# Transposing q and k whole in float32 and splitting them on the way out of PSUM, with keys of four blocks in one tile

## The chip, the cores and the metric

The kernel runs on one core of one Trainium2 chip. The metric is the device time of one execution in microseconds, the median over runs. The kernel before has a median of 1172.38 us in three runs (1171.7 to 1174.79 us).

## The reference, cut to what matters

One decoder block on 1024 tokens of width 1024. A modulated RMS norm feeds one input projection; its columns are split into queries, keys and values of two mixers. Mixer A has 8 query heads on 2 key heads with a window of 128 and a sink; mixer B has 8 heads, each the mixture of three dilated windows. Both outputs are normed and go through one output projection; then a squared-ReLU MLP follows. Everything is float32.

```python
h = rms_norm(x, g_attn_pre[l]) * (1 + sc_a) + sh_a
proj = h @ w_in[l]
qa = partial_rope(proj[..., :o1].reshape(b, s, A_Q_HEADS, HEAD_DIM), cos, sin)
ka = partial_rope(proj[..., o1:o2].reshape(b, s, A_KV_HEADS, HEAD_DIM), cos, sin)
va = proj[..., o2:o3].reshape(b, s, A_KV_HEADS, HEAD_DIM)
qb = partial_rope(proj[..., o3:o4].reshape(b, s, B_HEADS, HEAD_DIM), cos, sin)
kb = partial_rope(proj[..., o4:o5].reshape(b, s, B_HEADS, HEAD_DIM), cos, sin)
vb = proj[..., o5:].reshape(b, s, B_HEADS, HEAD_DIM)
oa = banded_attention(qa.reshape(b, s, A_KV_HEADS, A_GROUP, HEAD_DIM), ka, va, A_WINDOW - 1, sink=sink_a[l])
ob = dilated_mixture_attention(qb, kb, vb).reshape(b, s, B_W).astype(x.dtype)
mixed = jnp.concatenate([rms_norm(oa, g_mix_a[l]), rms_norm(ob, g_mix_b[l])], axis=-1)
y = mixed @ w_out[l]
x = x + gt_a * rms_norm(y, g_attn_post[l])
h = rms_norm(x, g_mlp_pre[l]) * (1 + sc_m) + sh_m
y = jnp.square(jax.nn.relu(h @ w_up[l])) @ w_down[l]
x = x + gt_m * rms_norm(y, g_mlp_post[l])
```

The scores are `q · k / 8` (head width 64); the kernel computes a window's scores with a mask that is added to them.

## The kernel before

**Split numbers.** A float32 number is held as a high part in the matmul's reduced type (`fp32r`) and a low part, the rest. A projection product takes three matmuls (high by high, high by low, low by high; L766, L767, L769). For the scores the two parts of q stand one above the other on the 128 partitions, 64 for the high and 64 for the low part of one head, and are the stationary operand; the keys' high part stands twice on the 128 partitions, and so does their low part. So two matmuls, one with the keys' high and one with their low parts, give the whole product.

**Stages.** From 0 to about 60 us the modulation is computed, x is normed and transposed, and the first projection unit begins. From about 61 to 455 us projection and attention run interleaved. Then come the output projection, and from about 545 us the MLP, which is the longest part (L1797 to L1799).

**Units and tiles.** The input projection has six units of 384 columns: units 0 to 3 hold two heads of mixer B each (2 q, 2 k, 2 v), units 4 and 5 one key head of mixer A each (4 q, 1 k, 1 v). Each unit runs over 8 token blocks of 128, so there are 48 tiles. A tile is 24 matmuls of 384 columns into a PSUM bank `pj` (`acc` in unit 0). `evac(u, tb, ...)` takes it from there:

- `f_vh`, `f_vl`: v is split (ACT, then DVE);
- `f_rope`: the rotary part, on DVE, in the bank itself;
- `f_h`, `f_l`: q and k are split in token order, high parts on ACT (L706, L707), low parts on DVE (L711, L712), into `sp` and `sk`; the bank is then free;
- `f_pq`: q goes through transposes in `fp32r`, one for each head (L719), into the PSUM bank `px`; `f_q` copies each out on ACT, times -1/8 (L724);
- `f_pk`: k goes through two transposes a head (L731) into `px` again; `f_k` copies them out to a key tile `kt` on ACT or DVE, whichever the planner expects to end earlier (L745). In units 4 and 5 each key block is copied a second time for the next block's tile (L756).

So a tile has six transposes in two groups, and `px`, a single bank, is taken twice. A key tile holds 256 keys: two blocks in units 0 to 3, the block before and its own in units 4 and 5.

**Attention items.** `s_b` does the scores of a pair of query blocks of one B head (all keys so far, in PSUM pieces of up to 512 and matmuls of up to 256 columns, L1022), `s_a_` those of one query block of four A heads (L1073). Then DVE adds the mask and takes the minimum (L1040, L1089), ACT takes the exponential (L1047, L1094), the probabilities are scaled (L1052 on POOL, L1111 on POOL or DVE), transposed in float32 (L1125, L1128, L1132), split (L1139 on ACT, L1143 on DVE) and multiplied by v (L1156 to L1161, L1167).

**What sets the order.** No order is written out. `Sched` plans while the program is built: each step has a duration in the source (`t_ps`, `t_dv`, a number), dependencies, and counted resources (`r_x` for the bank `px`, `r_k` and `r_q` for key and query buffers). It places steps on five in-order queues at the times that it expects; PE takes its streams in the order of `prefer()`, transposes of q and k (`post`) first. On the chip the queues run in that order, whatever the durations turn out to be. So a changed duration or resource in the source moves instructions on all engines.

## Time and profile before

| what | value |
|---|---|
| median of the runs | 1172.38 us |
| the profiled execution's own time | 1175.14 us |
| its span, first to last instruction | 1173.3 us |
| granted TensorE clock, mean | 0.993 |
| PE busy, by the page | 1137.0 us, 97% |
| DVE, ACT, POOL busy, by the page | 74%, 58%, 20% |
| stretch of projection and attention | about 61 to 455 us |

How to read it: the execution's time is 1.84 us over its span, and it is 2.76 us over the median of the runs. A matmul's duration in the trace includes its way through the array, so that one starts before the one ahead has ended; what a matmul costs in a row of others is the distance from one start to the next, and that is read from the timeline. PE's busy share therefore tells when PE waits, not how fast it works.

### The profile page before, as it was taken

To read this page: it belongs to the slowest core of one execution; us is meant where nothing else is said; L and a number is where in the kernel's file an instruction comes from. 1 tells how busy PE (TensorE), PEld (TensorE's weight loads), DVE (VectorE), ACT (ScalarE), POOL (GpSimd) and SP (SyncE) were. 2 spreads that over 40 slices of the span, in tenths; PEclk is the share of its full clock that TensorE was granted. 3 is DMA by queue.
4 is the path that set the end of the run, shared out by engine and by line. 5 is a ranking of instruction groups with operands and counts; after the bars stand their busy time and mean duration, and the time that the engine had idled before them with its cause. 6 is when DMAs were issued, how large, how long until landed. Compare 5 with 4: busy or idle time off the path is not lost.

```text
span 1173.3 us, 17394 instructions
## 1 busy us (share of the span) xinstructions
PE 1137.0 (97%) x6042; PEld 987.6 (84%) x6042; DVE 871.9 (74%) x1765; ACT 677.6 (58%) x1421; POOL 239.3 (20%) x295
## 2 busy tenths in 40 slices
PE   8999999999999999999899999999999999999996
PEld 7889999999988878887688888888888888888885
DVE  7876787776788896668969764499653796636998
ACT  7966676666666786666667524473225733246542
POOL 2053464554654451112000000000000000000002
PEclk9999999999999999999999999999999999999998
DMA  9712234132223224465485147922258411575103
GB/s 327 209 64 78 74 87 117 53 104 71 70 70 104 79 73 130 172 202 218 150 333 181 36 150 243 357 84 90 100 214 306 143 50 54 202 283 201 37 19 144
DMA packets 96488, 166.54 MB, mean 142 GB/s; under 512 B 11408, under 2 KB 48400, under 8 KB 96400
## 3 DMA queue, kind: packets, MB, share of 16 engines
q1 hardware_dynamic: 96400, 165.42, 42.0%
q8 instruction: 48, 0.79, 0.3%
q14 instruction: 40, 0.33, 0.1%
HBM read 137.08 MB, written 28.31 MB: 141 GB/s over the span
## 4 chain that ended last, share of the span: by engine, by line
PE 77%; DVE 11%; issue 4%; ACT 3%; POOL 1%; DMA 1%; DVEq 0%; POOLq 0%; SPq 0%; ACTq 0%
PE mlp_ps L1798 16%; PE mlp_ps L1799 16%; PE mlp_ps L1797 16%; PE pj L766 4%; PE pj L767 4%; PE pj L769 4%; PE s_ps L1022 3%; PE o_ps L1156 2%; PE pt_ps L1125 1%; DMA w_st<-in_w_in 1%; PE y_ps L1373 1%; PE y_ps L1375 1%; PE y_ps L1374 1%; PE s_ps L1073 1%; PE pt_ps L1128 1%
## 5 line engine op out<-in xcount | busy, mean ns | idle before, releaser
L1797 PE MATMUL mlp_ps<-hw 128*128 128x512 f32 x896 | 349.7, 390 | 1.1 <-ACT hw L1559 1.1
L1798 PE MATMUL mlp_ps<-hw 128*128 128x512 f32 x896 | 348.7, 389 | 1.1 <-DVE hw L1565 1.1
L1799 PE MATMUL mlp_ps<-hw 128*128 128x512 f32 x896 | 348.6, 389 | 0.0
L1797 PEld LDWEIGHTS mlp_ps<-hw 128*128 128x128 f32 x896 | 168.2, 188 | 36.9 <-ACT hw L1559 1.6
L1798 PEld LDWEIGHTS mlp_ps<-hw 128*128 128x128 f32 x896 | 168.2, 188 | 36.6 <-DVE hw L1565 1.4
L1799 PEld LDWEIGHTS mlp_ps<-hw 128*128 128x128 f32 x896 | 168.2, 188 | 34.9
L1568 DVE TENSOR_TENSOR hw<-w,hw 128x1024 fp32r<-128x1024 f32 x96 | 114.6, 1219 | 95.1 <-ACT hw L1561 93.0
L1561 ACT CAST hw<-w 128x1024 fp32r<-128x1024 f32 x96 | 97.4, 1046 | 129.9 <-PE mlp_ps L1799 93.2
L1897 POOL TENSOR_TENSOR st<-st,nhalf 128x1 f32<-128x1 f32 x8 | 7.7, 977 | 602.0 <-DVE st L1895 602.0
L766 PE MATMUL pj<-w_hl,hw 128*128 128x384 f32 x320 | 119.1, 372 | 0.0
L767 PE MATMUL pj<-w_hl,hw 128*128 128x384 f32 x320 | 108.7, 340 | 0.5 <-DVE w_hl L506 0.5
L769 PE MATMUL pj<-w_hl,hw 128*128 128x384 f32 x320 | 108.9, 340 | 0.0
L1561 ACT CAST hw<-u 128x1024 fp32r<-128x1024 f32 x48 | 48.6, 1052 | 64.6 <-PE mlp_ps L1799 64.6
L1143 DVE TENSOR_TENSOR ph<-pt_ps,ph 128x512 fp32r<-128x512 f32 (+1 forms) x110 | 68.9, 644 | 18.6 <-ACT ph L1139 18.0
L1568 DVE TENSOR_TENSOR hw<-u,hw 128x1024 fp32r<-128x1024 f32 x48 | 57.0, 1218 | 18.2 <-ACT hw L1561 18.2
L1139 ACT CAST ph<-pt_ps 128x512 fp32r<-128x512 f32 (+1 forms) x110 | 59.8, 562 | 12.9 <-PE pt_ps L1128 8.8
L1052 POOL TENSOR_SCALAR p_sb<-p_sb,den 128x128 f32<-128x128 f32 (+3 forms) x64 | 49.1, 773 | 87.4 <-DVE den L1050 49.8
L1855 DVE TENSOR_TENSOR yacc<-yacc,mlp_ps 128x512 f32<-128x512 f32 x96 | 62.2, 681 | 3.3 <-PE mlp_ps L1799 3.3
L767 PEld LDWEIGHTS pj<-w_hl,hw 128*128 128x128 f32 x320 | 61.0, 191 | 2.1 <-DVE w_hl L506 0.8
L766 PEld LDWEIGHTS pj<-w_hl,hw 128*128 128x128 f32 x320 | 60.7, 190 | 1.6 <-issue 0.5
L769 PEld LDWEIGHTS pj<-w_hl,hw 128*128 128x128 f32 x320 | 60.6, 189 | 0.0
L1047 ACT ACTIVATE p_sb<-p_sb,mn 128x128 f32<-128x128 f32 (+3 forms) x64 | 50.0, 782 | 17.4 <-DVE mn L1040 13.5
(206 smaller groups left out, 2201.0 us busy)
## 6 DMA issues: line engine op xcount, KB each, us to landing
hw<-s_dram SPq DMA_DIRECT2D x84, 512.0 KB, 4.4
wa_st<-in_w_ada SPq DMA_DIRECT2D x32, 512.0 KB, 4.2
w<-in_w_up SPq DMA_DIRECT2D x32, 512.0 KB, 5.1
w<-in_w_down SPq DMA_DIRECT2D x32, 512.0 KB, 7.5
s_dram<-hw SPq DMA_DIRECT2D x28, 512.0 KB, 4.5
x_sb<-in_x SPq DMA_DIRECT2D x16, 512.0 KB, 5.4
wa<-in_w_ada SPq DMA_DIRECT2D x32, 256.0 KB, 6.1
w_st<-in_w_in SPq DMA_DIRECT2D x32, 192.0 KB, 3.8
```

Of the source, the lines that this page charges most:

```text
L766: T.matmul(ps, hw[:, tb, 0, t], w[:, 0], start=(k == 0), stop=False)
L767: T.matmul(ps, hw[:, tb, 0, t], w[:, 1], start=False, stop=False)
L769: T.matmul(ps, hw[:, tb, 1, t], w[:, 0], start=False, stop=(k == KC - 1))
L1047: A.activation(rec.p[qi], rec.p[qi], AF.Exp, bias=b["mn"][:, m:m + 1], scale=-1.0, accum_out=b["den"][:])
L1139: A.copy(b["ph"][:, 0, :w], b["pt"][:, :w])
L1143: V.tensor_tensor(b["ph"][:, 1, :w], b["pt"][:, :w], b["ph"][:, 0, :w].bitcast(F32), ALU.subtract)
L1561: A.copy(out[j][0], flat(src[j]))
L1568: V.tensor_tensor(out[j][1], flat(src[j]), out[j][0].bitcast(F32), ALU.subtract)
L1797: T.matmul(ps[m][:], sh, mh, start=starts and k == 0, stop=False, **kw)
L1798: T.matmul(ps[m][:], sh, ml_, start=False, stop=False, **kw)
L1799: T.matmul(ps[m][:], sl, mh, start=False, stop=k == 3, **kw)
L1855: e = op("DVE", t_dv(512), lambda: V.tensor_tensor(y(), y(), ps[m][:], ALU.add), [e, ml.e_y[tb, n]], gives=gives, prio=1)
```

## The change

**Transposes.** `f_h` now copies q and k of a tile in float32 to one buffer `sq`: three groups of 128 columns, each a pair of q heads, or one k head twice. `f_l` is gone. `f_pq` transposes the three groups in float32 into `px`, once. Out of PSUM, `f_q` copies the high parts of q on ACT (two instructions, 64 partitions each), `f_ql` the low parts on DVE, as a `scalar_tensor_tensor` whose output lies on the other 64 partitions (two instructions); `f_k` copies the keys' high parts on ACT, and `f_kl` takes the low parts on DVE, one instruction a k head each. `f_kn`, the second copy of A's keys, is gone. The bank `pj` is given free after this copy on ACT, and no longer after DVE's low parts of q and k.

**Scores.** A key tile holds four blocks, 512 keys (`kts[u, tb // 4, h]`). A B score product takes all of a piece's columns at once, up to 512. An A block finds its 256 keys side by side in a tile, but for block 4, whose two key blocks lie in two tiles: there each head takes four matmuls of 128 columns in place of two of 256.

**Planner.** Buffers are counted by the new tiles (`NK` 6 of twice the size, `NQ` 4 of four times), the duration of a dense projection step is 0.52 in place of 0.49, that of a score step 0.014 + 2 · max(0.1, 0.00043 · columns).

```diff
-    WR, WS, NP, NV, NK, NQ, NT, NO = 10, 5, 4, 21, 10, 12, 2, 6
+    WR, WS, NP, NV, NK, NQ, NT, NO = 10, 5, 4, 21, 6, 4, 2, 6
...
         def f_h():
-            t.sp = prp.tile([P, 4, 2, 64], F32R, name="sp", tag="sp", bufs=2)
-            t.sk = prp.tile([P, 2, 2, 2, 64], F32R, name="sk", tag="sk", bufs=2)
-            b["kd"] = b["prv"][:, nq:].unsqueeze(2).to_broadcast([P, nk, 2, 64])
-            A.copy(t.sp[:, :nq, 0], b["prv"][:, :nq])
-            A.copy(t.sk[:, :nk, 0], b["kd"])
-        e5 = op("ACT", t_as(64 * nq) + t_as(128 * nk), f_h, [e3], takes=[(r_sp, 1)], prio=2)
-
-        def f_l():
-            V.tensor_tensor(t.sp[:, :nq, 1], b["prv"][:, :nq], t.sp[:, :nq, 0].bitcast(F32), ALU.subtract)
-            V.tensor_tensor(t.sk[:, :nk, 1], b["kd"], t.sk[:, :nk, 0].bitcast(F32), ALU.subtract)
-        e6 = op("DVE", t_dv(64 * nq) + t_dv(128 * nk), f_l, [e5, t.e_v], gives=[(r_bank, 1)], prio=2)
+            t.sq = prp.tile([P, 3, 2, 64], F32, name="sq", tag="sq", bufs=2)
+            A.copy(t.sq[:, :n2], b["prv"][:, :nq].rearrange("p (x e) d -> p x e d", e=2))
+            A.copy(t.sq[:, n2:n2 + nk], b["prv"][:, nq:].unsqueeze(2).to_broadcast([P, nk, 2, 64]))
+        e5 = op("ACT", t_as(64 * nq) + t_as(128 * nk), f_h, [e3, t.e_v], takes=[(r_sp, 1)], gives=[(r_bank, 1)], prio=2)
...
-            b["pq"] = px.tile([P, 4, P], F32R, name="pq", tag="x")
-            for h in range(nq):
-                T.transpose(b["pq"][:, h], t.sp[:, h].rearrange("p s d -> p (s d)"), ident_r[:])
-        e7 = pe_op("post", 0.056 * nq, f_pq, [e6, e_idr], takes=[(r_x, 1), (r_q, nq)])
+            b["pq"] = px.tile([P, 3, P], F32, name="pq", tag="x")
+            for x_ in range(3):
+                T.transpose(b["pq"][:, x_], t.sq[:, x_].rearrange("p e d -> p (e d)"), ident)
+        e7 = pe_op("post", 0.327, f_pq, [e5], takes=[(r_x, 1), (r_q, int(new_q)), (r_k, nk if new_k else 0)], gives=[(r_sp, 1)])
...
         def f_q():
-            for h in range(nq):
-                A.mul(t.q[h][:], b["pq"][:, h].bitcast(F32), -0.125)
-        t.e_q = op("ACT", nq * t_ps(128), f_q, [e7], gives=[(r_x, 1)], prio=2)
+            for e in range(2):
+                src, dst = of(0, e)
+                A.mul(dst[64 * e:64 * e + 64], src, -0.125)
+        eq = op("ACT", 2 * t_ps(128 * n2), f_q, [e7], prio=2)
+
+        def f_ql():
+            for e in range(2):
+                src, dst = of(0, e)
+                V.scalar_tensor_tensor(dst[64 - 64 * e:128 - 64 * e], src, -0.125,
+                                       dst[64 * e:64 * e + 64].bitcast(F32), ALU.mult, ALU.subtract)
+        t.e_q = op("DVE", 2 * t_dv(128 * n2), f_ql, [eq], prio=2)
...
-        e8 = pe_op("post", 0.112 * nk, f_pk, [e6], takes=[(r_x, 1), (r_k, need_k)], gives=[(r_sp, 1)])
...
+        ek = op("ACT", nk * t_ps(128), f_k, [e7], prio=2)
+        t.e_k = op("DVE", nk * t_dv(128), f_kl, [ek, t.e_q], gives=[(r_x, 1)], prio=2, after=posted)
...
-            d = dense(0.49, emit, [w_e[u, k]] + [], takes=[(r_pj, 1)] if k == 0 else [], gives=gives, after=tick)
+            d = dense(0.52, emit, [w_e[u, k]] + [], takes=[(r_pj, 1)] if k == 0 else [], gives=gives, after=tick)
...
-                    for b0 in range(0, cw, 256):
-                        w = min(256, cw - b0)
-                        for hl in range(2):
-                            T.matmul(s[:, b0:b0 + w], toks[u, qb].q[h][:],
-                                     kts[u, (c0 + b0) // 256, h][:, hl, :w], start=(hl == 0), stop=(hl == 1))
-                d = 0.218 * -(-cw // 256)
+                    for hl in range(2):
+                        T.matmul(s[:, :cw], toks[u, qb].q[h], kts[u, m, h][:, hl, :cw], start=(hl == 0),
+                                 stop=(hl == 1))
+                d = 0.014 + 2 * max(0.1, 0.00043 * cw)
...
-                kt = kts[u, qb, 0]
+                x_ = qb % 4
+                keys = [(qb // 4, 0 if x_ == 0 else (x_ - 1) * P, x_ * P + P, k0 if x_ else P)]
+                if x_ == 0 and qb:
+                    keys.append((qb // 4 - 1, 3 * P, 4 * P, 0))
                 for hh in range(2):
-                    for hl in range(2):
-                        T.matmul(s[:, hh, k0:], toks[u, qb].q[2 * j + hh][:], kt[:, hl, k0:],
-                                 start=(hl == 0), stop=(hl == 1))
+                    for i_, a_, z_, o_ in keys:
+                        for hl in range(2):
+                            T.matmul(s[:, hh, o_:o_ + z_ - a_], toks[u, qb].q[2 * j + hh], kts[u, i_, 0][:, hl, a_:z_],
+                                     start=(hl == 0), stop=(hl == 1))
```

**Where instructions move.** The rows below are the programs' own, in their order on one engine. First PE in unit 3, around the transposes of q and k of token block 4, before: `pq` and `pk` are the two groups of transposes, `pj` the projection, `pt_ps` the probabilities' transposes.

```order
L1022 MATMUL s_ps<-kt,qt 128x256 x4
L719 MATMUL pq<-ident_r,sp 128x128 x2
L766 MATMUL pj<-w_hl,hw 128x384
L767 MATMUL pj<-w_hl,hw 128x384
L769 MATMUL pj<-w_hl,hw 128x384
L1125 MATMUL pt_ps<-head,p_sb 128x128 x2
L1128 MATMUL pt_ps<-head,p_sb 128x128
L731 MATMUL pk<-ident_r,sk 128x128 x4
```

The same block's transposes on PE in the change, and a little ahead of them two score products of 384 and 512 columns:

```order
L1023 MATMUL s_ps<-kt,qt 128x384 x2
L769 MATMUL pj<-w_hl,hw 128x384
L770 MATMUL pj<-w_hl,hw 128x384
L772 MATMUL pj<-w_hl,hw 128x384
L1023 MATMUL s_ps<-kt,qt 128x512 x2
...
L727 MATMUL pq<-head,sq 128x128 x3
L1130 MATMUL pt_ps<-head,p_sb 128x128 x2
L1133 MATMUL pt_ps<-head,p_sb 128x128 x2
L769 MATMUL pj<-w_hl,hw 128x384
```

Two groups of transposes with other work between them have become one group of three, and pairs of matmuls of 256 columns have become single ones of up to 512.

Next DVE at block 1 of unit 3, before: the split of v, then of q and k (`sp`, `sk`), then attention's own work.

```order
L684 TENSOR_TENSOR v_hl<-pj,v_hl 128x64 x2
L711 TENSOR_TENSOR sp<-pj,sp 128x2x64
L712 TENSOR_TENSOR sk<-pj,sk 128x2x128
L1143 TENSOR_TENSOR ph<-pt_ps,ph 128x512
L1143 TENSOR_TENSOR ph<-pt_ps,ph 128x384
L1040 ISA p_sb,mn<-s_ps,masks 128x512
```

And in the change, for the same block, where `qt` and `kt` are the low parts of q and k behind the transposes:

```order
L743 SCALAR_TENSOR_TENSOR qt<-pq,qt 64x128 x2
L1041 ISA p_sb,mn<-s_ps,masks,mn 128x384
L1041 ISA mn 128x1
L1196 TENSOR_TENSOR ot<-o_ps,otmp 64x256
L1041 ISA p_sb,mn<-s_ps,masks 128x512
L1041 ISA mn 128x1
L756 TENSOR_TENSOR kt<-pq,kt 128x128 x2
```

The low parts have moved from ahead of the transposes to behind them, and the keys' stand behind two steps of the softmax.

Last PE at block 4 of unit 5, before and in the change: its score products.

```order
L1073 MATMUL s_ps<-kt,qt 128x256 x4
L766 MATMUL pj<-w_hl,hw 128x384
L767 MATMUL pj<-w_hl,hw 128x384
L769 MATMUL pj<-w_hl,hw 128x384
L1073 MATMUL s_ps<-kt,qt 128x256 x4
```

```order
L1078 MATMUL s_ps<-kt,qt 128x128 x8
L769 MATMUL pj<-w_hl,hw 128x384
L770 MATMUL pj<-w_hl,hw 128x384
L772 MATMUL pj<-w_hl,hw 128x384
L727 MATMUL pq<-head,sq 128x128 x3
L1078 MATMUL s_ps<-kt,qt 128x128 x8
```

Four matmuls of 256 columns have become eight of 128, twice.

On PE the first 310 instructions, up to the first transposes of q, and the last 3103, from within the first output blocks on, stand in the same order as before. On the way, the planner also moves the split of the output projection's weight: all eight pieces are on DVE in the change (L1256), four of them were on POOL (L1256 and L1257 before); and 32 low parts of the input projection's weight are on POOL, where 26 were (L506).

57 lines of the change are left out of this document (26 added, 31 removed).

## The prediction

> **What bounds the kernel now.** The page comes first, for the shares of the engines; then the windows, for the one stretch that the change touches; then the waits of PE there; then the timeline of PE, for what a matmul costs.
>
> ```profile
> span 1173.3 us, 17394 instructions
> PE 1137.0 (97%) x6042; PEld 987.6 (84%) x6042; DVE 871.9 (74%) x1765; ACT 677.6 (58%) x1421; POOL 239.3 (20%) x295
> ```
>
> PE is nearly always at work. The programs' order says that the first 310 PE instructions and the last 3103 stand as before; in the trace they lie on both sides of the stretch below. So the MLP and the start can give or take nothing, and the change is decided in between:
>
> ```profile
> 340.00:430.00 90.00, 84.14 (x540) 79.29 (x538) 78.90 (x268) 67.77 (x229) 41.19 (x58) 0.96 0.27 82
> 61.00:455.00 394.00, 379.52 (x2607) 359.62 (x2606) 304.21 (x1049) 269.82 (x843) 200.23 (x241) 0.99 0.28 79
> ```
>
> The columns are the stretch, its length, then busy time of PE, weight loads, DVE, ACT and POOL. In these 394 us PE is idle for 394.0 - 379.5 = 14.5 us only. Whatever PE no longer has to do there should come off the time, as long as the other engines keep up: DVE is busy for 304.2 us, 77% of the stretch, and for 88% of the part from 340 to 430 us, which belongs to mixer A. That part is the place to be careful. Who makes PE wait today:
>
> ```profile
> PE pq L719 <- DVE sp L711: 3.7, 3, 2.2
> PE pk L731 <- ACT qt L724: 1.2, 2, 0.7
> PE pq L719 <- ACT sk L707: 0.8, 1, 0.8
> ```
>
> These are waits at the transposes of q and k, 5.7 us in all: for the split in front of them, and for `px` between the two groups.
>
> **The transposes on PE.** A start-to-start distance in the timeline is a price.
>
> ```profile
> 72.35 0.46 PE L731 MATMUL pk<-ident_r,sk 128*128 128x128 f32 x4
> 72.64 0.41 PE L766 MATMUL pj<-w_hl,hw 128*128 128x384 f32 x1
> 72.88 0.33 PE L767 MATMUL pj<-w_hl,hw 128*128 128x384 f32 x1
> ...
> 74.30 0.29 PE L719 MATMUL pq<-ident_r,sp 128*128 128x128 f32 x2
> 74.42 0.41 PE L766 MATMUL pj<-w_hl,hw 128*128 128x384 f32 x1
> 74.67 0.34 PE L767 MATMUL pj<-w_hl,hw 128*128 128x384 f32 x1
> ```
>
> ```profile
> 358.40 0.60 PE L1132 MATMUL pt_ps<-head,p_sb 128*128 128x128 f32 x4
> 358.75 0.42 PE L766 MATMUL pj<-w_hl,hw 128*128 128x384 f32 x1
> 359.01 0.34 PE L767 MATMUL pj<-w_hl,hw 128*128 128x384 f32 x1
> ...
> 359.36 0.64 PE L1073 MATMUL s_ps<-kt,qt 128*128 128x256 f32 x4
> 359.83 0.33 PE L766 MATMUL pj<-w_hl,hw 128*128 128x384 f32 x1
> ...
> 360.71 0.34 PE L769 MATMUL pj<-w_hl,hw 128*128 128x384 f32 x1
> 363.24 0.51 PE L719 MATMUL pq<-ident_r,sp 128*128 128x128 f32 x4 [2.19 <-DVE sp L711]
> ```
>
> From 359.83 to 360.71 five projection matmuls start: 0.176 us for 384 columns. The matmul behind a group of transposes takes longer than that, so I price a group up to the start of the second matmul behind it, less one 0.176. The four `pk`: 72.88 - 72.35 - 0.176 = 0.354. The two `pq`: 74.67 - 74.30 - 0.176 = 0.194. Together 0.548 us a tile; A's tiles have four and two, the same six in two groups, and I take the same. The new transposes are float32 by the float32 identity, as the probabilities' four at 358.40 are: 359.01 - 358.40 - 0.176 = 0.434, so three cost 0.326. That saves 0.222 a tile, and with 48 tiles **10.7 us**.
>
> Here a rule speaks against the change. A plain float32 product does cost several times a reduced one in this trace:
>
> ```profile
> 179.12 1.02 PE L925 MATMUL ada_ps<-ada_acc,ones 128*128 128x512 f32 x2
> 179.58 0.74 PE L766 MATMUL pj<-w_hl,hw 128*128 128x384 f32 x1
> 180.16 0.33 PE L767 MATMUL pj<-w_hl,hw 128*128 128x384 f32 x1
> ```
>
> One float32 product of 512 columns stands there as two records, and takes 180.16 - 179.12 - 0.176 = 0.86 us. The Trainium skill's page "FP8 and Floating Point Precision", section "TensorE Precision Notes", says that true float32 goes through the array in four passes; the 0.86 us agree with that. By that rule alone three transposes would cost 3 x 0.86 / 4 = 0.65 us a tile, more than today's six. But the float32 transposes at 358.40 are one record each at 0.109 us, and the new ones have their form, so I go by them.
>
> **The score products.**
>
> ```profile
> 253.89 0.33 PE L1022 MATMUL s_ps<-kt,qt 128*128 128x128 f32 x2
> 254.06 0.39 PE L766 MATMUL pj<-w_hl,hw 128*128 128x384 f32 x1
> 254.29 0.34 PE L767 MATMUL pj<-w_hl,hw 128*128 128x384 f32 x1
> ```
>
> ```profile
> 465.76 0.39 PE L1373 MATMUL y_ps<-hw,oh 128*128 128x512 f32 x1
> 465.98 0.39 PE L1374 MATMUL y_ps<-hw,oh 128*128 128x512 f32 x1
> 466.21 0.39 PE L1375 MATMUL y_ps<-hw,ol 128*128 128x512 f32 x1
> ```
>
> Pairs (keys' high and low): 128 columns 254.29 - 253.89 - 0.176 = 0.224; 256 columns (359.83 - 359.36) / 2 = 0.235; 384 columns 2 x 0.176 = 0.352; 512 columns 466.21 - 465.76 = 0.45. For a B head, the query blocks 2 and 6 have a piece of 384 columns, 0.235 + 0.224 = 0.459 now and 0.352 then: twice 0.107. Six pieces have 512 columns (blocks 3, 4, 5, 6 and twice 7), 0.47 now and 0.45 then: six times 0.02. That is 0.334 a head, 2.7 us for eight heads. Against it, A's block 4 needs two pairs of 128 in place of one of 256: 0.448 - 0.235 = 0.213 for each of eight heads, 1.7 us. The products together save **1.0 us**: wider matmuls are the smaller half of the change by far, since 256 columns were already nearly at the pace of 512.
>
> **The other engines.** DVE's work, removed and added:
>
> ```profile
> L712 DVE TENSOR_TENSOR sk<-pj,sk 128x256 fp32r<-128x256 f32 x24 | 9.9, 413 | 0.0
> L745 DVE CAST kt<-pk 128x256 fp32r<-128x256 f32 x23 | 9.0, 417 | 4.0 <-PE pk L731 3.9
> L711 DVE TENSOR_TENSOR sp<-pj,sp 128x128 fp32r<-128x128 f32 x24 | 6.8, 285 | 5.1 <-ACT sk L707 4.9
> L711 DVE TENSOR_TENSOR sp<-pj,sp 128x256 fp32r<-128x256 f32 x16 | 6.6, 412 | 0.6 <-ACT sk L707 0.6
> L756 DVE CAST kt<-pk 128x256 fp32r<-128x256 f32 x9 | 3.7, 413 | 0.0
> L1143 DVE TENSOR_TENSOR ph<-pt_ps,ph 128x512 fp32r<-128x512 f32 x78 | 52.1, 683 | 13.6 <-ACT ph L1139 13.1
> L1394 DVE SCALAR_TENSOR_TENSOR y_sb<-y_ps,rab,y_sb 128x512 f32<-128x512 f32 x16 | 11.8, 747 | 8.1 <-PE y_ps L1375 7.9
> L1251 DVE SCALAR_TENSOR_TENSOR hw<-wo_st,head,hw 128x1024 fp32r<-128x1024 f32 x4 | 5.1, 1282 | 1.2 <-ACT hw L1248 1.2
> ```
>
> Removed, with unit 0's eight tiles at the prices of units 1 to 3: 32 x 0.285 + 16 x 0.412 for q, 32 x 0.413 + 16 x 0.285 for k, 9.0 + 3.7 of copies, 46.2 us. Added: 80 low parts of keys, 128 columns, 0.285 each, 22.8; and 96 `scalar_tensor_tensor` on 64 partitions, an operation that no row has in this size. Its price lies between that of a `tensor_tensor` of as many columns (0.285 for 64, 0.412 for 32: 31.4 in all) and that of the 512-column row (0.747 each: 71.7). I take the nearer end, with the 0.747 - 0.683 = 0.064 that the one operation costs over the other at 512 columns: 64 x 0.349 + 32 x 0.476 = 37.6. So DVE gets 22.8 + 37.6 - 46.2 = 14.2 us more (8 to 48), and the four pieces of output weight that leave POOL are 4 x 1.282 = 5.1 more (six low parts of the input weight go the other way, from DVE to POOL; I leave them out). The stretch then asks DVE for 304.2 + 19.3 = 324 us out of 394 - 11.7 = 382, 85%; even at the upper end 358, 94%. It still fits, so I count nothing for it as a sum, but each place where DVE runs late becomes likelier to reach PE. ACT makes 14 instructions fewer in all and is at 269.8 of 394 us; POOL loses more work than it gets. No DMA is added or taken away.
>
> **What is late next.** The transposes stop waiting for DVE's split: at 363.24 PE had stood for 2.19 us behind that queue. That wait is not gone, it moves: the score products now need low parts that DVE makes behind the transposes, and `px` stays taken until the last of them. In the change's DVE order the two q parts of a block stand ahead of, and its key parts behind, two steps of the softmax; behind a late key part wait the block's first score products and the next holder of `px`. Between the bounds, all 5.7 us of the old waits gone or as much again in new ones, I take 1 us lost.
>
> **How the numbers follow.** The profiled execution took 1175.14 us: less 10.7, less 1.0, plus 1.0 is 1164.4. It was 2.76 us over the median of the runs, 1172.38, so against that the same sum gives **1161.7 us**.
>
> - *The forecast* (0.55): 1158 to 1165.
> - *The old waits go and nothing takes their place* (0.13): another 5.7 + 1.0 off, 1155. For it: the transposes need ACT alone now. Against: the low parts have to be made all the same.
> - *DVE becomes the bound in mixer A's part* (0.22): DVE has 78.9 us of work in those 90, and with four 1.28 us pieces of weight 84. PE's share of the gain there, 14 tiles x 0.222 = 3.1, is lost, and up to 5.1 us of new work show: 1165 to 1170, at 1167. For it: 88% busy, and the row at 363.24. Against: the tensor steps there nearly balance, as the second key copies go.
> - *Slower: every tile waits for its low part* (0.07). One mechanism: the first score product of a tile stands until DVE has done one more 0.349 us step than it had to. 48 x 0.349 = 16.8 against 11.7 gives 5.1 us more than before, 1177.5; it decides from 0.24 us a tile on. For it: the keys' part stands behind softmax steps in DVE's order. Against: score products wait for almost nothing today, and PE has projection matmuls ahead of most of them.
> - *The transposes take four passes* (0.01): (0.65 - 0.548) x 48 = 4.9 more, less 1.0: 1176.3. The rows at 358.40 speak against it.
> - *The change does not reach PE* (0.02), because the planner puts other waits where the work was: 1172. The order speaks against it: 288 transposes are 144, 448 score matmuls 336.
>
> Differences under 0.3%, 3.5 us, can't be told from none here. Faster by more takes in the first two and most of the third, 0.84; within it lie the rest of the third and the last, 0.08; slower 0.08. The range, 1154.5 to 1170, reaches from the vanished waits to the end of the DVE case.
>
> **What would show it.** The three float32 transposes at 0.33 us a tile and no second group; score matmuls of 512 at 0.22 to 0.23; the stretch, from the first q transposes to the last `o_ps`, shorter by 10 to 12 us; PE idle there near 15 us; DVE near 85%. I would be wrong if PE's waits for `qt` or `kt` add up to more than 4 us, if its waits in A's part double, or if a `scalar_tensor_tensor` takes over 0.6 us.

## The result, and the profile after

The changed kernel takes 1180.03 us (median of 6 runs, 1179.18 to 1181.24); the kernel before, run beside it, 1172.04 us (6 runs, 1170.9 to 1176.92). The ratio is 1.0061, with a 95% interval of 1.0041 to 1.0082: **slower by 0.6%**, where 0.9% faster was forecast. The profiled execution of the changed kernel took 1180.52 us.

First the page of the changed kernel, its first lines:

```profile
span 1178.7 us, 16924 instructions
PE 1132.8 (96%) x5786; PEld 973.1 (83%) x5786; DVE 879.7 (75%) x1810; ACT 680.8 (58%) x1407; POOL 235.9 (20%) x294
```

PE has 256 instructions fewer in the records and is busy for less time, yet the span is longer. Next the windows, as in the prediction: stretch, length, busy PE, weight loads, DVE, ACT, POOL, granted clock, DMA share, GB/s. The changed kernel:

```profile
61.00:459.00 398.00, 374.14 (x2353) 344.42 (x2352) 311.15 (x1091) 271.72 (x829) 197.59 (x241) 0.98 0.28 78
340.00:430.00 90.00, 85.09 (x519) 78.18 (x517) 79.63 (x268) 69.40 (x212) 37.95 (x55) 0.96 0.27 77
64.00:170.00 106.00, 95.11 (x601) 85.92 (x601) 83.89 (x314) 71.37 (x235) 49.04 (x58) 1.00 0.22 64
...
420.00:460.00 40.00, 33.32 (x178) 28.05 (x177) 30.54 (x92) 28.75 (x72) 7.63 (x16) 0.91 0.22 60
```

The kernel before, for the stretches that the prediction did not look at:

```profile
64.00:170.00 106.00, 102.36 (x725) 97.32 (x725) 79.31 (x297) 71.99 (x230) 51.28 (x61) 0.98 0.24 71
...
420.00:460.00 40.00, 36.84 (x209) 30.67 (x210) 32.01 (x94) 30.30 (x81) 16.72 (x22) 1.00 0.31 85
```

Mixer A's part, 340 to 430 us, is as it was: PE stands there for 4.9 us, 5.9 before. The idle time is at the two ends. From 64 to 170 us PE stood for 3.6 us before and stands for 10.9 now; from 420 to 460 us it was 3.2 and is 6.7. What PE waits for from 64 to 170 us (in total, times, longest), in the changed kernel:

```profile
PE pq L727 <- DVE kt L756: 3.0, 4, 1.8
PE o_ps L1161 <- DVE ot L1196: 2.0, 2, 1.6
PE pt_ps L1130 <- POOL p_sb L1053: 1.8, 1, 1.8
PE o_ps L1161 <- DVE ph L1148: 1.1, 3, 0.4
```

and before:

```profile
PE o_ps L1156 <- DVE ph L1143: 1.7, 4, 0.9
PE pq L719 <- ACT sk L707: 0.8, 1, 0.8
```

The first row is new: the transposes wait until DVE has made the last key low part of the tile ahead, because `px` is taken until then. The second is DVE late with something that has nothing to do with q and k.

**Work and waits apart.** PE's busy time hides short waits. So I take the starts of PE's matmuls from the timeline, the distance from each to the next, and subtract the 20th percentile of the distances between two matmuls of the same kinds and widths in all the traces of this study. What is over by more than 0.1 us counts as waiting, everything else as work. From the first transposes of q to the last product with v, both kernels having 33 matmuls of the output projection in it:

| | before | after |
|---|---|---|
| work | 361.9 us | 350.6 us |
| waits | 27.8 us | 42.8 us |
| of these, up to 170 us | 9.0 | 16.9 |
| 170 to 420 us | 13.8 | 15.8 |
| from 420 us | 5.1 | 10.0 |
| waits of the products with v | 11.3 | 21.7 |
| waits of q's and k's transposes | 8.2 | 9.6 |
| waits of the score products | 2.0 | 3.7 |

So 11.3 us of work are gone, as forecast (11.7), and 15.0 us of waits have come, two thirds of them in front of the products with v, which the change doesn't touch.

### The profile page after: what moved, and what is told of

Read it like the earlier page. It is cut to its first block, busy times and chain, and to the rows that moved or that the text cites. A ratio compares the mean times of both kernels' runs of the same rounds, so it can differ in the third digit from the quotient of the medians.

```text
span 1178.7 us, 16924 instructions
## 1 busy us (share of the span) xinstructions
PE 1132.8 (96%) x5786; PEld 973.1 (83%) x5786; DVE 879.7 (75%) x1810; ACT 680.8 (58%) x1407; POOL 235.9 (20%) x294
## 4 chain that ended last, share of the span: by engine, by line
PE 71%; DVE 12%; issue 5%; DMA 4%; ACT 4%; POOL 2%; SPq 1%; DVEq 0%; POOLq 0%; ACTq 0%
PE mlp_ps L1803 16%; PE mlp_ps L1802 16%; PE mlp_ps L1804 16%; PE pj L769 3%; PE pj L772 3%; PE pj L770 3%; PE s_ps L1023 2%; DMA wa<-in_w_ada 2%; PE o_ps L1161 1%; DVE p_sb L1041 1%; PE y_ps L1378 1%; PE y_ps L1380 1%; PE y_ps L1379 1%; PE pq L727 1%; PE o_ps L1172 1%
## 5 line engine op out<-in xcount | busy, mean ns | idle before, releaser
L1804 PEld LDWEIGHTS mlp_ps<-hw 128*128 128x128 f32 x896 | 168.5, 188 | 35.1
```

The costliest lines, as they stand in the source:

```text
L1804: T.matmul(ps[m][:], sl, mh, start=False, stop=k == 3, **kw)
```

## Experiments

Each number is a median; each ratio is to runs of the kernel before on the same chip. Every kernel was profiled, and the table of work and waits made for it. Where a kernel has more or fewer than 33 output matmuls in the stretch, its work is brought to 33 at 0.228 us each.

### The planner's pace, and the end of the stretch

The first suspect was the order: the change also raises the planned duration of a projection step. Two kernels move that number alone, a third the load that stands in front of PE's longest wait, a fourth does both.

```diff
-            d = dense(0.52, emit, ...
+            d = dense(0.49, emit, ...
```

> The changed kernel with one number put back: the planner's duration of a dense projection step is 0.49 again in place of 0.52. No instruction is added or removed on PE; only the order moves. Theory P (the longer planned step makes the plan run PE at its true pace, so that ACT's and DVE's steps, which the plan takes for shorter than they are, lose the slack that the too fast plan gave them, and PE now waits in small pieces from 72 to 170 us): most of the lost 16 us comes back, 1164 to 1170 us, and PE's waits from 72 to 170 us fall from about 9 us to under 4. Theory C (the new split itself costs the waits: px is held until the last low part on DVE, whatever the plan says): unchanged, 1177 to 1181 us. Theory T (only the end of the stretch is at fault, where the load of the first output block stands behind a wait for DVE's last piece of output weight): the 4.9 us stand at 435 us decides; with it gone 1174 to 1176 us, with it there 1180.

1180.8 us, 1.0051 (1.0034 to 1.0068): as slow as the changed kernel, and its waits up to 170 us are about 18 us, no fewer than there.

> The kernel before with one number of the change alone: the planner's duration of a dense projection step is 0.52 in place of 0.49. Same instructions on PE. Theory P: slower than before by 4 to 12 us, 1176 to 1184 us, with more PE waits from 72 to 170 us. Theories C and T: within 3 us of the kernel before, 1169 to 1175 us.

1175.68 us, 1.0016 (1.0001 to 1.0030), some 2 us slower than before, at no more waits up to 170 us (about 8 us). Theory P falls on both sides: the pace does not make the loss.

The end. These rows of the changed kernel's timeline (start, duration, engine, line; the wait ahead in brackets) belong together:

```profile
431.07 1.28 DVE L1256 SCALAR_TENSOR_TENSOR hw<-wo_st,head,hw 128x1024 fp32r<-128x1024 f32 x1
...
432.38 0.33 SPq L1277 DMA_DIRECT2D gate_a<-gate_d  x1
432.81 0.38 SPq L1323 DMA_DIRECT2D o_sb<-o_dram  x1
...
437.49 1.04 ACT L1336 CAST oh<-o_sb 128x1024 fp32r<-128x1024 f32 x1 [3.87 <-DMA o_sb<-o_dram]
...
439.06 0.58 ACT L1207 COPY otmp<-o_ps 64x512 f32<-64x512 f32 x1
...
440.57 1.73 PE L1172 MATMUL o_ps<-ph,v_hl 128*128 128x512 f32 x3 [4.94 <-DVE ot L1212]
```

SP's load waits for the memory of the last piece of output weight, which DVE finishes at 432.35; ACT stands in its order until the load has landed; behind it stands the copy that frees `po`; PE stands for 4.94 us. The planner knows nothing of the first link.

```diff
-[e_mod[0], e_mod[1]], prio=-7)
+[e_mod[0], e_mod[1]] + list(ph2.e_wo.values()), prio=-7)
```

> The changed kernel, where the load of gate_a is told to the planner as depending on all pieces of output weight, so that it is queued on SP behind the first load of o_sb and no longer ahead of it. Theory T: the 4.9 us stand of PE at 435 us goes or shrinks to about 1 us, and the time falls by 3 to 5 us, to 1175 to 1177 us. Theories P and C: the end of the stretch is a small part or another wait takes its place, 1178 to 1181 us; the waits before 320 us must stay as they are under all three.

1178.36 us, 1.0037 (1.0025 to 1.0049). The wait shrinks to 3.8 us only: o_sb, now the first to use that memory, waits in gate_a's place.

> Both edits of the two kernels on the changed kernel: dense step planned at 0.49, and gate_a queued behind the first o_sb load. Theory P with T: 1160 to 1167 us, about what was forecast for the change. Theory P alone: as with 0.49 alone, 1164 to 1170. Theory C: 1175 to 1177 by the end of the stretch alone.

1177.47 us, 1.0028 (1.0014 to 1.0041). Waits of 41.5 us: P with T falls. The wait at 435 us is 3.5 us here too, by another cause: one piece of output weight went to POOL, and DVE stood for as long as POOL worked on it.

```profile
434.24 2.32 DVE L1106 TENSOR_TENSOR es<-mn,head 128x4 f32<-128x4 f32 x1
...
434.18 2.36 POOL L1262 TENSOR_TENSOR hw<-wo_st,hw 128x1024 fp32r<-128x1024 f32 x1
```

Then the load of o_sb, too, was told to the planner as depending on the weight:

```diff
+        if tb == 0:
+            deps = deps + list(ph2.e_wo.values())
         el = load(f_lo, 524288, deps, ...
```

> The changed kernel, where the planner is told that the first load of o_sb and that of gate_a must wait for all pieces of output weight (as they do on the chip, for the memory). ACT's conversion of that block then stands later in its order. Theory T in its second form (ACT stands in its order at the conversion of o_sb, and the copies behind it hold the bank that the next products with v need): PE's longest wait at 435 us falls under 2 us, 1175 to 1178 us. If the wait there stays at 3 to 5 us, another engine's order is at fault, 1178 to 1181.

1177.3 us, 1.0023 (1.0012 to 1.0033). PE's longest wait at the end is 2.0 us, the waits from 420 us fall from 10.0 to 6.2, and those up to 170 us stay at 16.9. Against the changed kernel's 1.0061 that is about 4 us. So the end holds a third of the new waits (5.1 us of 15.0: all waits together fall from 42.8 to 37.7), and the rest is elsewhere. I call this one the mended kernel. The three kernels that come next are built on the changed kernel, all later ones, but for the doubling in the kernel before, on the mended one.

### The split behind the transposes

In the changed kernel, a tile's way through `px` reads like this (timeline, all engines):

```profile
162.56 0.49 PE L727 MATMUL pq<-head,sq 128*128 128x128 f32 x3
...
163.09 0.57 ACT L737 ACTIVATE qt<-pq 64x128 fp32r<-64x128 f32 x2 [0.20 <-PE pq L727]
...
163.67 0.44 ACT L752 CAST kt<-pq 128x128 fp32r<-128x128 f32 x2
...
164.14 0.59 DVE L743 SCALAR_TENSOR_TENSOR qt<-pq,qt 64x128 fp32r<-64x128 f32 x2 [0.42 <-ACT kt L752]
...
164.74 0.49 DVE L756 TENSOR_TENSOR kt<-pq,kt 128x128 fp32r<-128x128 f32 x2
```

ACT's four copies, then DVE's four low parts, one after the other: the bank is held for 2.7 us where nothing is late, and for a median of 3.2 us up to 340 us. Before, the two holders of a tile took 0.9 and 1.2 us (medians, again up to 340 us). DVE's row has a wait for the key copies, though it reads q. What DVE waits for from 61 to 459 us, after:

```profile
DVE qt L743 <- ACT kt L752: 14.5, 20, 1.8
```

and before, in front of the steps that these replace:

```profile
DVE sp L711 <- ACT sk L707: 6.2, 11, 0.6
...
DVE kt L745 <- PE pk L731: 3.9, 8, 1.0
```

The first try issues q's low parts ahead of the key copies.

```diff
         def f_k():
+            f_ql()
             for h in range(nk):
                 A.copy(k_at(h)[:, 0], ...
```

> The changed kernel, where the low parts of q are issued before the copies of the keys' high parts, so that ACT raises its semaphore behind the two q copies and DVE need not stand until the key copies are done. Same instructions. In the changed kernel DVE stands 14.5 us in all in front of the low parts of q until ACT has copied the keys. Theory D (the in-order DVE is what PE waits for: the probabilities' low parts and the output copies stand behind this wait, and PE's products with v wait for them): DVE's idle time there falls to under 5 us, PE's waits of the products with v for DVE fall by 3 to 6 us, 1174 to 1177 us. Theory H (the hold of the bank px, from the transposes to the last low part, is what costs): the hold gets shorter by only 0.3 us a tile, 1178 to 1181 us. Under both the end of the stretch may move by some us, since the planner puts the pieces of output weight elsewhere; it is read apart.

1185.57 us, 1.0098 (1.0083 to 1.0114): worse, and against both theories. The groups of the lines view (out, in, shapes, count; busy, mean ns; idle before, its cause) tell why:

```profile
L754 ACT CAST kt<-pq 128x128 fp32r<-128x128 f32 x80 | 18.1, 268 | 42.2 <-DVE qt L743 42.0
```

Now ACT stands, for 42 us in all. The program lets ACT and DVE at a bank only in turn, in the order in which it was written, even where both only read; the wait was turned round. This has a reason that no run here touches: the Trainium skill's page "PSUM — Partial Sum Buffer", section "PSUM bank collisions raise a hardware error", says that two engines on the same bank and quadrant at once raise an error, reads included. So as long as both work on the same partitions the chain on `px` has to be serial. Whether ACT on one half of the partitions and DVE on the other could go side by side, no run tried.

Two kernels take the bank out of it: ACT copies all of `px` to SBUF and frees it; the parts are made from that copy, on DVE as now, or on POOL.

```diff
+        def f_raw():
+            t.raw = prp.tile([P, 3, P], F32, name="raw", tag="raw", bufs=2)
+            A.copy(t.raw[:], b["pq"][:])
+        er = op("ACT", t_ps(384), f_raw, [e7], takes=[(r_raw_, 1)], gives=[(r_x, 1)], prio=2)
```

> The changed kernel with one more step a tile: ACT copies all three transposed groups in float32 from px to a buffer in SBUF, which frees the bank, and the high and low parts are made from the buffer. 48 ACT copies of 384 columns more, some 17 us of ACT work; DVE's work stays as it is. Theory H: px is free 0.5 to 1.2 us behind the transposes in place of 3.2 (median), PE's waits at the transposes go, 1171 to 1176 us. Theory D: DVE has as much to do and waits for ACT as before, no gain, 1179 to 1184 us.

1201.39 us, 1.0231 (1.0213 to 1.0248). Freeing the bank in this way does not help, and H's time falls. But DVE's steps got dearer, so that its work did not stay as I had said, and the run cannot tell what the bank alone is worth:

```profile
L762 DVE TENSOR_TENSOR kt<-raw,kt 128x128 fp32r<-128x128 f32 x79 | 32.1, 439 | 0.5
L749 DVE SCALAR_TENSOR_TENSOR qt<-raw,qt 64x128 fp32r<-64x128 f32 x64 | 32.0, 501 | 8.6 <-ACT qt L743 6.8
```

They took 0.282 and 0.289 us out of PSUM. With the 64x256 group DVE has 29 us more of these, and ACT has 23 us of copies more (48 of 0.482 us); PE's waits rise from 42.8 to 62.3 us.

The same with POOL making the low parts (the copy of q is scaled by -1/8 on the way, so that POOL only subtracts):

```diff
-        t.e_q = op("DVE", 2 * t_dv(128 * n2), f_ql, ...
+        t.e_q = op("POOL", 2 * t_ptt(128 * n2), f_ql, ...
-        t.e_k = op("DVE", nk * t_dv(128), f_kl, ...
+        t.e_k = op("POOL", nk * t_ptt(128), f_kl, ...
```

> As the kernel with the copy to SBUF, but all low parts of q and k are made on POOL (GpSimd) from it, 96 + 80 instructions that leave DVE. DVE then has some 50 us less to do in the stretch than in the changed kernel. Theory D: the products with v stop waiting for DVE's low parts, 1168 to 1174 us, if POOL, which gets some 80 us more, doesn't become late with the probabilities' scaling. Theory H: as with the copy alone, 1171 to 1176. If both fall, POOL's own lateness shows as waits of PE for p_sb and qt, 1180 or more.

1175.21 us, 1.0012 (1.0001 to 1.0024): faster than the changed kernel by some 6 us, though ACT has 25 us more to do from 61 to 459 us (297 for 272). DVE is busy there for 273 us, 311 in the changed kernel. Waits fall by 7.7 us, to 35.1; score products wait now, 8.7 us, among others for POOL's key parts. The time misses theory D's range and lies in H's. Since `px` is freed early here too, this run does not separate DVE's load from the hold of the bank.

That kernel with the mended end:

```diff
+            deps = deps + list(ph2.e_wo.values())
```

> The kernel with low parts of q and k on POOL, with the first o_sb load planned behind the output weight. If the two gains add up (4 us from POOL, 2.5 from the end): 1170 to 1173 us, at or below the kernel before. If the end of the stretch there has another cause, 1175.

1177.31 us, 1.0028 (1.0015 to 1.0040): the gains do not add up. The waits from 420 us are 11.0 us here, for causes I did not follow up.

### One half alone, and one unit alone

The old split in token order, with its two groups of transposes, but keys of four blocks and wide score products:

```diff
-            b["pq"] = px.tile([P, 3, P], F32, name="pq", tag="x")
-            for x_ in range(3):
-                T.transpose(b["pq"][:, x_], t.sq[:, x_].rearrange("p e d -> p (e d)"), ident)
+                for h in range(nq):
+                    T.transpose(b["pq"][:, h], t.sp[:, h].rearrange("p s d -> p (s d)"), ident_r[:])
...
+                    for s in range(2):
+                        T.transpose(b["pk"][:, 2 * h + s], t.sk[:, h, s].rearrange("p e d -> p (e d)"), ident_r[:])
```

> One half of the change alone: keys of four blocks side by side and score products of up to 512 columns as in the changed kernel, but q and k are split in token order and transposed in two groups as before (with the new buffers; A's keys are copied once), and the first o_sb load planned behind the output weight. PE work is that of the changed kernel plus 11 us for the transposes. Theory S (the new split behind the transposes makes the other engines later, and that costs PE the 15 us): PE's waits of over 0.1 us between the first q transposes and the last product with v come back to 26 to 30 us in all (42.6 in the changed kernel, 27.7 before) and the time is 1168 to 1173 us. Theory W (the wider scores or the new order at large brings the waits): waits of 36 us or more, 1180 to 1186 us.

Waits of 28.5 us, work of 362.1: **undoing the split brings both back** to where they were before. This kernel has the mended end, so it is to be held against the mended kernel's waits, 37.7 us: the new split, with the order that the planner makes for it, brings 9.2 us of them, and the wider scores bring none. S holds, W falls. The time, 1176.33 us, 1.0024 (1.0008 to 1.0040), misses S's range, however. In the profiled execution the stretch is as long as before (389.9 and 389.7 us), but its first transposes come 1.2 us later and three output matmuls fewer lie inside it; the rest I can't account for. The time is also that of the mended kernel (1.0024 and 1.0023): the new split's saved work, 11 to 12 us, and its 9 us of waits nearly cancel. The wide scores by themselves bring nothing that shows.

The old split for unit 0 only:

```diff
+        if u == 0:
+            (the old split, as above)
```

> The changed kernel with the old split for unit 0 alone (its 8 tiles are evacuated closest together, every 2 us of projection in place of 4); units 1 to 5 have the new split; o_sb planned as in the run with the mended end. Theory S in its local form (the new split is too slow only where tiles come that fast): waits from the first q transposes to 170 us fall from 16.9 to 10 to 13 us, 1171 to 1175 us. If the whole split is at fault wherever attention runs: waits there fall by less than 2 us, 1176 to 1180.

1175.1 us, 1.0011 (0.9999 to 1.0022). Waits up to 170 us are 11.3 us, in place of 16.9, as the local form of S said. The time, some 1.4 us under the mended kernel's by the ratios, is not clear of the noise.

The planner was then told how long the two q steps take:

```diff
-        eq = op("ACT", 2 * t_ps(128 * n2), f_q, [e7], prio=2)
+        eq = op("ACT", 2 * (t_ps(128 * n2) + 0.122), f_q, [e7], prio=2)
-        t.e_q = op("DVE", 2 * t_dv(128 * n2), f_ql, [eq], prio=2)
+        t.e_q = op("DVE", 2 * (t_dv(128 * n2) + 0.1), f_ql, [eq], prio=2)
```

> The kernel with the mended end, and the planner is told what the two q steps take on the chip: 0.283 us for each ACT copy of 64 partitions by 128 (it plans 0.161) and 0.298 for DVE's low part (0.199). No instruction changes. If PE waits because the plan sends the next transposes before px is really free: waits at the transposes fall from 9 us to under 6, 1172 to 1175 us. If the time of the split itself is what is missing, the order can't give it back: 1176 to 1179 us.

1172.33 us, 0.9993 (0.9977 to 1.0009). The transposes wait 7.3 us in place of 9.1, not under 6, and all waits together hardly fall (37.3 from 37.7). The time came out below what they explain.

### What a microsecond of DVE costs

Here the order of every engine was left as it was and DVE was given work that changes no result: a low part computed twice.

```diff
                 V.tensor_tensor(k_at(h)[:, 1], b["pq"][:, n2 + h], ...)
+                V.tensor_tensor(k_at(h)[:, 1], b["pq"][:, n2 + h], ...)
```

> The kernel with the mended end, where each key low part is computed twice on DVE, the second over the first (80 instructions more, 0.2 us each start to start, 16 us of DVE in the stretch); the planner isn't told, so that the order on every engine is the same. Theory N (DVE's free share is no cover: what DVE gets more in the stretch comes through to PE in large part, as its steps lie in the chain from the transposes to the products): 1183 to 1193 us, 0.4 to 1 us for each us. Theory K (there is cover, as the prediction counted): 1176 to 1179 us.

1194.22 us, 1.0171 (1.0145 to 1.0198), 4 runs: 16.9 us over the mended kernel's median (17 by the ratios). But DVE got more than the 16 us that were expected. The same tile's key low parts in the mended kernel, and here:

```profile
68.12 0.48 DVE L756 TENSOR_TENSOR kt<-pq,kt 128x128 fp32r<-128x128 f32 x2
```

```profile
68.84 0.28 DVE L756 TENSOR_TENSOR kt<-pq,kt 128x128 fp32r<-128x128 f32 x1
69.16 0.29 DVE L757 TENSOR_TENSOR kt<-pq,kt 128x128 fp32r<-128x128 f32 x1
69.37 0.28 DVE L756 TENSOR_TENSOR kt<-pq,kt 128x128 fp32r<-128x128 f32 x1
69.68 0.29 DVE L757 TENSOR_TENSOR kt<-pq,kt 128x128 fp32r<-128x128 f32 x1
```

A step that writes again what the one ahead has just written starts 0.32 us behind it, where low parts of two heads start 0.20 us apart. Four such steps take 1.13 us in place of 0.48, and over all tiles these steps keep DVE busy for 46.0 us in place of 20.0, 26 us more. So a microsecond of DVE cost PE about 0.65. The waits rise from 37.7 to 55.0 us, and they do so at steps that were not doubled, too (waits of PE from 61 to 459 us):

```profile
PE pq L727 <- DVE kt L757: 7.1, 6, 2.4
PE o_ps L1162 <- DVE ph L1149: 4.5, 11, 1.1
PE o_ps L1162 <- DVE ot L1197: 4.2, 4, 1.6
```

In the kernel before:

```diff
             V.tensor_tensor(t.sk[:, :nk, 1], b["kd"], ...)
+            V.tensor_tensor(t.sk[:, :nk, 1], b["kd"], ...)
```

> The kernel before, where the low part of k in token order is computed twice on DVE (48 instructions more, 0.33 us each for two heads, 0.2 for one, 14 us in all), with the same order. Theory N: slower by 5 to 14 us, 1178 to 1188 us: the kernel before had no cover either. Theory U (the kernel before had cover, which the new split has used up): within 3 us of the kernel before, while the kernel with the doubled key low parts loses 8 us or more.

1179.25 us, 1.0051 (1.0033 to 1.0068): about 6 us. The doubled steps do not overlap here either and took about 20 us, not 14, so a microsecond cost 0.3: between N and U.

In the mended kernel again, ahead of the transposes:

```diff
                 V.tensor_tensor(t.v[h][:, 1], get_ps()[:, n + 64 * h:n + 64 * h + 64], ...)
+                V.tensor_tensor(t.v[h][:, 1], get_ps()[:, n + 64 * h:n + 64 * h + 64], ...)
```

> The kernel with the mended end, where the low part of every value tile is computed twice on DVE, the second over the first (80 instructions more, 0.138 us each start to start, 11 us in all), with the order of every engine left alone. These stand ahead of the transposes and don't touch px. Theory N (any microsecond more of DVE costs PE one): 8 to 11 us slower than the kernel with the mended end, 1185 to 1188 us. Theory X (it is the chain on px behind the transposes, ACT's four copies and then DVE's four steps on one bank, that has no cover; DVE elsewhere has some): 2 to 5 us slower, 1179 to 1182 us, as in the kernel before with its 14 us of doubled work.

1188.82 us, 1.0134 (1.0109 to 1.0158), 4 runs: 11.5 us over the mended kernel's median (13 by the ratios, either give or take 3). DVE got about 21 us, not 11, for the same reason, so this too is about 0.6 for each. X falls: work ahead of the transposes costs as much as work on `px`. N holds in kind, not in its full size: **with the new split a microsecond on DVE costs PE about 0.6, before it 0.3**.

That does not make it DVE's queue alone. The doubled steps all stand in a tile's own chain, these too, because ACT copies q and k out of the bank only behind DVE's low part of v (waits of ACT from 61 to 459 us, the mended kernel and this one):

```profile
ACT sq L707 <- DVE v_hl L684: 14.9, 18, 2.0
```

```profile
ACT sq L709 <- DVE v_hl L686: 24.6, 23, 2.4
```

No run doubled a DVE step for which no tile waits, so queue and chain are not told apart.

### A version that is faster than both

```diff
+        if u == 0:
+            (the old split)
...
+        eq = op("ACT", 2 * (t_ps(128 * n2) + 0.122), f_q, [e7], prio=2)
```

> Two edits that each helped, together: the old split in unit 0, and the planner told 0.283 and 0.298 us for the new q steps in units 1 to 5 (with the mended end). If they add up: waits of over 0.1 us from the first q transposes to the last product with v near 30 us (34.8 with the old split in unit 0, 37.3 with the durations), 1168 to 1172 us, under the kernel before. If the order chosen anew undoes it: 1173 to 1177.

**1170.3 us, 0.9975 (0.9961 to 0.9990)**: old split in unit 0, the true q durations, the mended end. It is below the kernel before by 0.25%, the clearest gain here (its interval leaves out 1, though the prediction took 0.3% as the least that can be told from none), and below the changed kernel by 0.9% (1.0061 to 0.9975). Waits 33.2 us, work 350.8.

With both key heads in one tile, and A's keys of a unit in one:

```diff
-            for h in range(nk):
-                V.tensor_tensor(k_at(h)[:, 1], b["pq"][:, n2 + h], k_at(h)[:, 0].bitcast(F32), ALU.subtract)
+            V.tensor_tensor(k_part(1), k_src(), k_part(0).bitcast(F32), ALU.subtract)
```

> The kernel with both remedies (old split in unit 0, the planner told of the q steps), and both key heads of a unit in one key tile, so that a tile's keys are copied by one ACT instruction and their low part made by one DVE instruction of 256 columns in place of two of 128; A's keys of a whole unit lie in one tile, so that block 4 needs no split of its score products. DVE and ACT each lose 24 instructions, 0.07 us each, 1.7 us; PE loses 1.7 us (16 score matmuls fewer, those of block 4). By theory N (a microsecond of DVE behind the transposes counts about whole): 1166 to 1169 us. If the keys now stay longer in their buffers (both heads are given back together) and the transposes of the next unit wait for that: 1171 us or more.

1171.15 us, 0.9986 (0.9973 to 0.9999). The last projection matmul starts at 413.7 us, 421.2 in the kernel above, but from 420 us on 11.0 us of waits take the gain back.

```diff
-        if u == 0:
+        if u < 2:
```

> As the kernel with one key tile, with the old split in units 0 and 1. PE gets 8 times 0.23 = 1.8 us of transposes back. If the new split costs in unit 1 as it does in unit 0: waits from 120 to 170 us fall from 4.5 us to about 2 and the time stays within 1 us of the other. If unit 0 was the only place: 1.5 to 2 us slower.

1173.33 us, 1.0006 (0.9993 to 1.0020), 2 us slower, and waits from 120 to 170 us are 3.2 us, 2.2 without (the 4.5 that the expectation starts from was measured in the kernel ahead of that one): unit 1 is no place where the new split loses.

## Why the prediction was wrong

**Right: what PE saves.** The three new transposes, in the changed kernel's timeline of PE:

```profile
214.82 0.49 PE L727 MATMUL pq<-head,sq 128*128 128x128 f32 x3
215.07 0.42 PE L769 MATMUL pj<-w_hl,hw 128*128 128x384 f32 x1
215.33 0.34 PE L770 MATMUL pj<-w_hl,hw 128*128 128x384 f32 x1
```

215.33 - 214.82 - 0.176 = 0.334 us, 0.328 in the median of ten such groups; forecast 0.326. Score products of 512 columns start 0.228 us apart, as said. The work fell by 11.3 us, forecast 11.7. The transposes make all of it: with the wide scores alone the work was that of before (362.1 and 361.9 us), so the 1.0 us of the products does not show. The four passes did not come.

**Too large: DVE's bill.** The new low parts:

```profile
L756 DVE TENSOR_TENSOR kt<-pq,kt 128x128 fp32r<-128x128 f32 x80 | 20.0, 282 | 0.6 <-ACT kt L752 0.3
L743 DVE SCALAR_TENSOR_TENSOR qt<-pq,qt 64x128 fp32r<-64x128 f32 x64 | 18.5, 289 | 13.0 <-ACT kt L752 11.9 <-ACT qt L737 0.3
...
L743 DVE SCALAR_TENSOR_TENSOR qt<-pq,qt 64x256 fp32r<-64x256 f32 x32 | 13.5, 422 | 4.0 <-ACT kt L752 2.6 <-ACT qt L737 0.7
```

`scalar_tensor_tensor` takes 0.289 and 0.422 us, less than the 0.349 and 0.476 that I took. Busy time is 52.0 us against 46.0 for the rows they replace, 6.0 more where 14.2 was forecast, with 8 as the lower bound. The weight came as said: eight pieces, 10.8 us, for four at 5.1. The low parts of the input weight that the prediction left out took 3.9 us off DVE (L506, 17.5 to 13.6 us). By the page DVE is busy for 7.8 us more in all (871.9 to 879.7), where 19.3 was forecast.

**Wrong: "It still fits, so I count nothing for it as a sum", and "I take 1 us lost".** These are the steps that failed: 15.0 us of new waits stood where the sum had 1. By the runs 5.1 us of them belong to the end of the stretch and 9.2 to the new split, which together leave 0.7. The 85% counts only the time in which DVE works. DVE goes through its queue in order, and where the first in it waits, all behind it wait: the new low parts make it stand for 17.6 us (0.6 + 13.0 + 4.0 in the rows above), where the old rows made it stand for 10.4. In the stretch as a whole, though, DVE is idle for no longer than before (from 61 to 459 us 86.9 us, 92.0 before), so what changed is where it stands and not how long. The runs with doubled work say that a microsecond more on DVE costs PE about 0.6 with the new split. At that price the 7.8 us more come to some 5 us (an estimate), and how the rest of the 9 us divides between DVE's queue and the longer hold of `px` stays open. I had named the waits that would move, and sought them at the two steps that I could name: the scores' first products, and `px`. The score products wait 1.7 us more, the transposes 1.4. It was the next customers of DVE that were late, the low parts of the probabilities and the sums `ot`, and behind them the products with v, 10.4 us more.

**Wrong: the place.** I looked at A's part, since DVE was 88% busy there; it has not changed. The waits came where tiles are evacuated fastest, unit 0 with the first attention items, and at the end. In the stretch from 64 to 170 us DVE was 75% busy before. The old split back in unit 0 took 5.6 us of waits away there.

**Half right: the rivals.** The slower rival (1177.5 us, a chance of 0.07) had the sign and nearly the size, by another mechanism: 0.35 us at each tile's first score product. Such a wait is not in the trace.

**Not in the prediction at all: the end.** The weight on DVE, priced at 5.1 us of DVE, ended up in front of a load, and through ACT's order in front of PE. Mending that was worth about 4 us. "No DMA is added or taken away" was true and not the question: one was moved behind a wait that the planner doesn't know of.

**The marks that I had set.** Stretch 10 to 12 us shorter: it is 3.6 us longer. PE idle near 15 us there: 23.9 of 398 us. DVE near 85%: 78% (311.15 of 398). PE's waits in A's part did not double, no `scalar_tensor_tensor` took over 0.6 us, and waits named after `qt` or `kt` add up to 3.0 us up to 170 us, 4.5 in all with the 1.5 us that a product of the modulation stood for `px`: just over the 4 us.

Open: why half the change alone is slower than before by 0.24% at equal waits, and why some kernels (the planner with the true q durations) are faster than their waits tell. The reasons why PE's waits at the end are now 5 and now 11 us were followed in two kernels only.

## What to carry to other kernels

An in-order engine's free share is no reserve: before counting more work on it at nothing, give it ten microseconds of work that changes no result, with the order left alone, read from the trace how much it really got, and see what comes through. A step moved behind a transpose moves onto a PSUM bank that ACT and DVE here read only in turn, so price how long the bank is held and who stands meanwhile. When a planner sets the order, look for the waits it doesn't know of (memory that is used again), since any change of the load can put a late one in front of the engine that counts.

## What the runs showed of the hardware

- **Alternate halves of the partitions, no overlap.** On 128 partitions one ACT copy starts 0.163 us after the last, though it takes 0.266, and DVE's low parts 0.207 after each other, at 0.290. The q steps, of which one reads the lower 64 partitions and the next the upper, start 0.283 (ACT) and 0.298 us (DVE) apart, which is their whole duration. It is not the 64 partitions as such: two `ot` sums of mixer A in a row, both on the same 64, start 0.341 us apart at a duration of 0.417. No run tells more of the cause. So two q heads' high parts hold ACT for 0.57 us, where two copies on 128 partitions, with twice the elements, would start 0.33 us apart in all.
- **DVE out of SBUF.** The key low part took 0.439 us with both operands in SBUF, 0.282 with one in PSUM, and a DVE step of 4 columns took 2.32 us while POOL was at a `tensor_tensor` of 2.36 us (rows above). The Trainium skill's page "SBUF — State Buffer", section "SBUF: two separate sides", says that the two share a port pair under a lock, which a DVE step with two SBUF inputs contends for; the rows agree, though no run here separated POOL from it.
- **The granted clock.** Runs of one kernel differ with it: the kernel with the true q durations took 1168.92 us at 0.997 and 1178.95 at 0.992. The dips differ from one profile to the next (0.91 from 420 to 460 us in the changed kernel's, 1.00 there before), so a few us in one profile may be theirs: 40 us at 0.91 in place of 1.00 are 3.6 us, as an estimate.
